# A trunk of two decoder layers on one core: the first group's queries and keys projected in one pass over the input tiles

## The chip, the cores and the metric

The kernel runs on one core of a Trainium2 chip. The metric is the device time of one execution in microseconds (us); the time of a kernel is the median of its runs. TensorE (PE) multiplies, VectorE (DVE), ScalarE (ACT) and GpSimd (POOL) do the rest, and all loads of the part that matters here are issued by SyncE (SP).

## What is computed

Two layers, 512 positions, width 1024, in float32. The first layer has stick-breaking heads and differential heads side by side, the second dilated attention; each layer ends in a squared-ReLU MLP and a gated embedding. Cut to what the change touches:

```
hn   = rmsnorm(h, norm_mix_g[i])
proj = hn @ w_in                      # 1024 -> 3072, split in qa, ka, va, qb, kb, vb
sc   = einsum('bqhmd,bkhmd->bhmqk', qb_b, kb) * scale
bias = table[t5_bucket(rel)]          # T5 bucket table, 32 x 16
prob = softmax(where(rel >= 0, sc + bias, NEG))
attn = prob[:, :, 0] - lam * prob[:, :, 1]
o_d  = rmsnorm(einsum('bhqk,bkhd->bqhd', attn, vb), subln_g) * (1 - lambda_init)
```

## The kernel before

Everything lies transposed: `h` is eight tiles of 128 channels x 512 positions. For float32 accuracy each operand is split in a high and a low part of type fp32r (`hi`/`lo` for inputs, `wh`/`wl` for weights; L187/L188, L122/L126/L128), and `mm3` (L141, L144, L145) forms three products: high x high, low x high, high x low. The high part is a copy on ACT, the low part a subtraction on DVE, or on POOL for weights of the mixer after the first blocks. The norm's factor is not applied to `h`; the products run on unnormed tiles, and the inverse root `rstd` is multiplied in when an accumulator is evacuated.

A layer's mixer works in four groups (`GROUPS`), each with 256 columns of queries, keys and values; `project` yields a group's products, `attend` the steps of its attention, and `interleave` writes the steps of one group among the products of the next. The first group (a differential one) has nothing to stand beside. Its order:

- The lead, at the level of `trunk`: SP loads `gcols`, then the eight input tiles and between them the queries' block in three chunks (1 MB); ACT and DVE split what has landed (L187, L188, L330, L331).
- `queries_keys`: two query accumulators over all eight tiles (`outer`, tile by tile), then `prepare`, then the key block (a load of its own, 1 MB, L114, split by L122 and L128) in two accumulators one after the other. Behind the first of them stands `statistics`: the squares (L250, L263) and two products with a matrix of ones (L272, L273), then the inverse root (L215 to L221).
- `prepare` makes the bias table: a product of the T5 table with one-hot rows (L351), written to DRAM (`urow`, L354), from where `load_bias` (L543) reads it with a shift.
- `evacuate` takes the four accumulators in turn: L495 multiplies by `rstd` into `tmp`, of which there is one buffer; for queries two copies and two subtractions follow (L501, L502), for keys four copies and two subtractions (L511 to L513).
- `values` (L447 on): the value block in two halves, the inverse root turned into columns before the second (`tok_cols`), four copies into `v` (L463, L464; tag "v", two buffers).
- The first `attend` steps stand among the value products of the second group: scores (L534, L535; two PSUM banks), softmax (L551, L554, L601 to L604).

Weight tiles have three buffers (tags "wh", "wl"), staging tiles two ("raw"). The lines of it that matter most:

```
start and isq: yield from lin_units(accs, blk, ahl, 0, KT, True)   # queries, tile by tile
prepare()
for i, acc in enumerate(accs):                                     # keys, one after the other
    yield from lin_units([acc], [blk[i]], ahl, 0, KT, False)
    if waiting:
        statistics()
        for x, held in enumerate(waiting):
            evacuate(True, x, held, qk, qscale)
```

The scheduler sets the order on each engine; it is printed below where the change moves it.

Of the kernel before, what the change touches and what calls it, by code (L numbers as in the profile page):

```python
# [12 lines left out]
F32 = mybir.dt.float32  # L13
# [6 lines left out]
P = 128  # L20
# [42 lines left out]
def trunk(  # L63
# [114 lines left out]
    def split_tile(src, scale=None, bufs=8, behind=()):  # L178
# [7 lines left out]
        else:  # L186
            last_split[:] = [nc.scalar.activation(hi, src, AF.Copy, scale=scale).ins]  # L187
            nc.vector.scalar_tensor_tensor(lo, src, scale, hi.bitcast(F32), op0=ALU.mult, op1=ALU.subtract)  # L188
# [126 lines left out]
    raw0 = wpool.tile([P, 2 * KT * P], F32, tag="raw", name=nm("raw"), bufs=2)  # L315
    raw0v = raw0.rearrange("p (i k c) -> p i k c", i=2, k=KT)
    src0 = w_in[0, 0].rearrange("p (i k c) -> p i k c", i=2, k=KT)
    blk0 = [tuple(wpool.tile([P, KT, P], F32R, tag=t, name=nm(t), bufs=3) for t in ("wh", "wl")) for _ in range(2)]
    chunks = {0: slice(0, 2), 1: slice(2, 4), 3: slice(4, 8)}
    nc.sync.dma_start(gcols, gvec)  # L320
    for k in range(KT):
        nc.sync.dma_start(h[k], xT[k])
        if k in chunks:
            nc.sync.dma_start(raw0v[:, :, chunks[k]], src0[:, :, chunks[k]])
    for k in range(KT):
        norm.done(k, stats=False)
        if k in chunks:
            for i, (hi, lo) in enumerate(blk0):
                ck = chunks[k]
                nc.scalar.activation(hi[:, ck], raw0v[:, i, ck], AF.Copy)  # L330
                nc.vector.tensor_tensor(lo[:, ck], raw0v[:, i, ck], hi[:, ck].bitcast(F32), op=ALU.subtract)  # L331
# [4 lines left out]
    def prepare():  # L336
        a, b, c, d = (mix[0].tile([P, S], F32, tag="bias", name=nm("prep"), bufs=4) for _ in range(4))
        lamt = t2k("tmp")[:, 0:4 * HD].rearrange("p (j c) -> p j c", j=4)
# [9 lines left out]
        for c0, src, offm in ((0, a[0:32], (b[0:16], c[0:16])),  # L348
                              (512, d[0:32, 0:128], (d[0:16, 128:256], d[0:16, 256:384]))):
            up = ps("pv" if c0 == 0 else "tp")[0:16, 0:src.shape[-1]]  # L350
            nc.tensor.matmul(up, d[0:32, 384:400], src, start=True, stop=True)  # L351
# [41 lines left out]
    def mixer(layer, norm, nxt):  # L393
# [12 lines left out]
        for t in pth + ptl:  # L406
            nc.gpsimd.memset(t[:, 11, :].bitcast(F32), 0.0)
        pt_i = [0]

        ahl = norm.parts()  # L410
        stat = {}

# [751 lines left out]
```

## Time and profile before

| | us |
|---|---|
| median of 3 runs (1294.65 to 1295.68) | 1295.13 |
| the profiled execution | 1294.86 |
| its span, first to last instruction | 1293.1 |
| PE busy | 1275.4 (99%) |
| DVE busy | 1003.9 (78%) |
| ACT busy | 709.5 (55%) |
| POOL busy | 212.9 (16%) |

The span is what the profile shows of the execution; some 1.8 us lie around it. Busy times are sums over instructions, and a busy engine need not be the one that sets the end: that is told by the chain that ended last and by what an engine waited for.

### The profile page before, as it was taken

The numbers are of one execution on the slowest core, as the hardware profiler recorded it, in microseconds if no ns is written. First come the engines' busy times: TensorE is split into PE (matmuls) and PEld (weight loads), VectorE is DVE, ScalarE is ACT, GpSimd is POOL, SyncE is SP. The second block draws the span as 40 slices with busy tenths as digits, with TensorE's granted clock in tenths as the row PEclk, the third lists the DMA queues.
The fourth block names the chain that finished last, engine by engine and source line by source line (L and its number), as shares of the span: only waits on it lengthen the run. The fifth ranks groups of instructions, "written<-read, shape, count | busy, mean of one in ns | idle before, by whom it ended". The sixth has DMA issues, their size and how long they took to land.

```text
span 1293.1 us, 19313 instructions
## 1 busy us (share of the span) xinstructions
PE 1275.4 (99%) x7520; PEld 1124.2 (87%) x7520; DVE 1003.9 (78%) x1666; ACT 709.5 (55%) x1146; POOL 212.9 (16%) x184
## 2 busy tenths in 40 slices
PE   9999999999999999999999999999999999999996
PEld 7988887888988989989889888788899898898986
DVE  6788798778848869779767777887785795986976
ACT  6667868555535335356456666765554443534544
POOL 2433434400000000001024333222000000000201
PEclk9999999999999999999999999999999999999999
DMA  6321423222222222638432222212323223255751
GB/s 211 144 82 54 159 75 114 90 98 98 95 102 98 98 98 98 195 107 219 140 127 86 82 90 75 73 58 80 116 98 101 95 99 115 82 148 146 173 178 66
DMA packets 33995, 144.25 MB, mean 112 GB/s; under 512 B 3888, under 2 KB 4624, under 8 KB 21232
## 3 DMA queue, kind: packets, MB, share of 16 engines
q1 hardware_dynamic: 29680, 135.16, 30.9%
q0 software_dynamic: 4224, 7.87, 3.6%
q8 instruction: 59, 0.97, 0.3%
q14 instruction: 32, 0.26, 0.1%
HBM read 131.92 MB, written 6.37 MB: 107 GB/s over the span
## 4 chain that ended last, share of the span: by engine, by line
PE 87%; DVE 7%; ACT 3%; issue 1%; DMA 0%; SPq 0%; POOL 0%; DVEq 0%; ACTq 0%; POOLq 0%
PE mm L141 11%; PE mm L144 11%; PE mm L145 11%; PE sc L144 6%; PE sc L145 6%; PE sc L141 5%; PE pv L145 5%; PE pv L144 5%; PE pv L141 5%; PE tp L145 4%; PE tp L144 4%; PE tp L141 4%; PE pv L581 3%; PE tp L560 2%; PE tp L900 2%
## 5 line engine op out<-in xcount | busy, mean ns | idle before, releaser
L122 ACT ACTIVATE wh<-raw 128x1024 fp32r<-128x1024 f32 (+1 forms) x156 | 160.5, 1034 | 142.6 <-PE mm L144 54.5
L126 POOL TENSOR_TENSOR wl<-raw,wh 128x512 fp32r<-128x512 f32 (+1 forms) x132 | 178.2, 1372 | 303.4 <-ACT wh L122 303.4
L141 PE MATMUL mm<-hi,wh 128*128 128x512 f32 x472 | 187.1, 396 | 0.6 <-DVE tmp L495 0.4
L145 PE MATMUL mm<-hi,wl 128*128 128x512 f32 x472 | 184.8, 391 | 0.1
L144 PE MATMUL mm<-lo,wh 128*128 128x512 f32 x472 | 184.6, 391 | 0.0
L128 DVE TENSOR_TENSOR wl<-raw,wh 128x1024 fp32r<-128x1024 f32 x90 | 109.5, 1223 | 39.6 <-ACT wh L122 34.1
L145 PEld LDWEIGHTS mm<-hi,wl 128*128 128x128 f32 x472 | 88.6, 188 | 20.0 <-POOL wl L126 0.5
L141 PEld LDWEIGHTS mm<-hi,wh 128*128 128x128 f32 x472 | 88.7, 188 | 17.5 <-DVE tmp L495 0.8
L144 PEld LDWEIGHTS mm<-lo,wh 128*128 128x128 f32 x472 | 88.8, 188 | 15.5
L784 POOL DMA_DIRECT2D s<-in_w_down_dram x4 | 4.5, 1123 | 578.7 <-DMA s<-in_w_down_dram 312.9
L813 ACT ACTIVATE wh<-s 128x1024 fp32r<-128x1024 f32 x58 | 61.1, 1054 | 54.5 <-DVE s L800 14.7
L554 ACT ACTIVATE e<-e,mn 128x128 f32<-128x128 f32 (+3 forms) x96 | 53.8, 561 | 62.5 <-DVE mn L551 62.2
L775 DVE TENSOR_TENSOR ul<-u,uh 128x1792 fp32r<-128x1792 f32 x32 | 64.8, 2024 | 29.4 <-ACT uh L774 29.2
L814 DVE TENSOR_TENSOR wl<-s,wh 128x1024 fp32r<-128x1024 f32 x58 | 70.9, 1222 | 16.6 <-ACT wh L813 16.3
L774 ACT ACTIVATE uh<-u 128x1792 fp32r<-128x1792 f32 x32 | 54.5, 1702 | 45.9 <-DVE u L772 45.9
L763 ACT ACTIVATE u<-u 128x512 f32<-128x512 f32 x64 | 39.7, 626 | 68.1 <-DVE u L762 68.1
L144 PE MATMUL sc<-lo,wh 128*128 128x512 f32 x184 | 72.0, 392 | 0.8 <-DVE lo L188 0.6
L141 PE MATMUL sc<-hi,wh 128*128 128x512 f32 x184 | 71.9, 391 | 0.7 <-ACT hi L187 0.7
L145 PE MATMUL sc<-hi,wl 128*128 128x512 f32 x184 | 71.8, 390 | 0.0
L141 PE MATMUL mm<-wh,hi 128*128 128x256 f32 (+1 forms) x216 | 63.3, 293 | 0.0
L145 PE MATMUL mm<-wh,lo 128*128 128x256 f32 (+1 forms) x216 | 63.0, 292 | 0.0
L144 PE MATMUL mm<-wl,hi 128*128 128x256 f32 (+1 forms) x216 | 62.9, 291 | 0.0
(308 smaller groups left out, 3884.5 us busy)
## 6 DMA issues: line engine op xcount, KB each, us to landing
raw<-in_w_up_dram SPq DMA_DIRECT2D x32, 1024.0 KB, 4.9
raw<-in_w_down_dram SPq DMA_DIRECT2D x32, 1024.0 KB, 4.9
raw<-in_w_in_dram SPq DMA_DIRECT2D x23, 1024.0 KB, 4.9
raw<-in_w_gate_dram SPq DMA_DIRECT2D x8, 1024.0 KB, 4.9
bias<-urow SPq DMA_DIRECT2D x24, 256.0 KB, 3.6
raw<-in_w_outa_dram SPq DMA_DIRECT2D x8, 768.0 KB, 4.2
pj<-pjd SPq DMA_DIRECT2D x16, 256.0 KB, 4.8
h<-in_xT_dram SPq DMA_DIRECT2D x8, 256.0 KB, 5.8
```

The lines of the kernel that those rows point to most:

```text
L122: act = nc.scalar.activation(hi, src, AF.Copy)
L126: nc.gpsimd.tensor_tensor(lo[:, kx], src[:, kx], hi[:, kx].bitcast(F32), op=ALU.subtract)
L128: last_low[:] = [nc.vector.tensor_tensor(lo, src, hi.bitcast(F32), op=ALU.subtract).ins]
L141: mm = nc.tensor.matmul(acc, lh, rh, start=start, stop=False)
L144: nc.tensor.matmul(acc, lh, rl, start=False, stop=False)
L145: return mm.ins, nc.tensor.matmul(acc, ll, rh, start=False, stop=stop).ins
L554: nc.scalar.activation(e[:, 0:n], e[:, 0:n], AF.Exp, scale=-1.0, bias=mn, accum_out=s)
L763: chain.append(nc.scalar.activation(ui, ui, AF.Square, scale=0.5).ins)
L774: nc.scalar.activation(uh, u, AF.Copy)
L775: part = nc.vector.tensor_tensor(ul, u, uh.bitcast(F32), op=ALU.subtract)
L813: high[:] = [nc.scalar.activation(hi, src, AF.Copy).ins]
L814: low[:] = [nc.vector.tensor_tensor(lo, src, hi.bitcast(F32), op=ALU.subtract).ins]
```

## The change

The first group's four weight blocks (two of queries, two of keys) are loaded in chunks between the input tiles, queries and keys in turn, and PE takes all four accumulators tile by tile. Two of the four split blocks lie in the buffers of the tag "v", in which the value tile follows later. `prepare` is cut in two: the loads and conversions stay ahead, and the product of the table, now in fp32r with the table split in high and low part, comes behind the 96 products of queries and keys, followed by `statistics`. The four evacuations come after that.

```
+    LOADS = (("h", 0, 1), ("w", 0, 2), ("h", 1, 2), ("w", 2, 4), ("h", 2, 4), ("w", 4, 8), ("h", 4, 8))
+    def lead_loads(mpool):
+        nc.sync.dma_start(gcols, gvec)
+        raws = [wpool.tile([P, 2 * KT * P], F32, tag="raw", name=nm("raw"), bufs=2) for _ in range(2)]
+        views, parts = [], []
+        for raw in raws:
+            views.append(raw.rearrange("p (k i c) -> p i k c", i=2, k=KT))
+            parts.append([wpool.tile([P, KT, P], F32R, tag=t, name=nm(t), bufs=3) for t in ("wh", "wl")])
+            both = mpool.tile([P, QT, 512], F32R, tag="v", name=nm("wv"), bufs=2).rearrange(
+                "p (x a) b -> p x (a b)", x=2).rearrange("p x (k c) -> p x k c", k=KT)
+            parts.append([both[:, x] for x in range(2)])
...
+        for what, a, b in LOADS:
+            if what == "h":
+                for k in range(a, b):
+                    nc.sync.dma_start(h[k], xT[k])
+            else:
+                cols = slice(a * 2 * P, b * 2 * P)
+                for x, raw in enumerate(raws):
+                    nc.sync.dma_start(raw[:, cols], w_in[0, x][:, cols])
+        for what, a, b in LOADS:
+            if what == "h":
+                for k in range(a, b):
+                    norm.done(k, stats=False)
+                    in_turn(*last_split)
+            else:
+                for x, (hi, lo) in enumerate(parts):
+                    src = views[x // 2][:, x % 2, a:b]
+                    act = nc.scalar.activation(hi[:, a:b], src, AF.Copy)
+                    in_turn(act.ins, nc.vector.tensor_tensor(lo[:, a:b], src, hi[:, a:b].bitcast(F32), op=ALU.subtract).ins)
+        return parts, list(ahead)
...
 def prepare():
-            nc.tensor.matmul(up, d[0:32, 384:400], src, start=True, stop=True)
...
+        nc.vector.tensor_copy(onr[0:32], a[0:32])
+        nc.vector.tensor_copy(endr[0:32, 0:128], d[0:32, 0:128])
+        nc.vector.tensor_copy(th, d[0:32, 384:400])
+        nc.vector.tensor_tensor(tl, d[0:32, 384:400], th.bitcast(F32), op=ALU.subtract)
...
+        def rest():
...
+                nc.tensor.matmul(up, th, src, start=True, stop=False)
+                nc.tensor.matmul(up, tl, src, start=False, stop=True)
...
 def queries_keys():
+                if start and not layer:
+                    rest = prepare()
+                    accs = [ps(lead_in.pop(0)) for _ in range(4)]
+                    yield from lin_units(accs, lead, ahl, 0, KT, True)
+                    rest()
+                    statistics()
+                    for i, acc in enumerate(accs):
+                        evacuate(i < 2, i % 2, acc, qk, qscale)
+                    return
...
             if start:
                 yield from queries_keys()
-                yield from values()
-            else:
-                yield from values()
+            v = value_tile()
+            cur.extend((g, kind, v, heads))
+            yield from values()
+            if not start:
                 yield from queries_keys()
```

The change moves instructions on the engines. Three places follow, of before first and of the change behind it; line numbers of the change are some 40 higher from `prepare` on.

First place: PE at the end of the first group's queries (before), and at the end of its queries and keys (after). `sc` are the query accumulators, `mm` the key accumulators, `pv` and `tp` banks for the table, the norm and the values, `hi`/`lo` numbers stand for input tiles.

```order
L141 MATMUL sc_208<-hi_173,wh_119 128x512
L144 MATMUL sc_208<-lo_174,wh_119 128x512
L145 MATMUL sc_208<-hi_173,wl_120 128x512
L351 MATMUL pv_281<-prep_269,prep_272 16x512
L351 MATMUL tp_287<-prep_272 16x128
L141 MATMUL mm_267<-hi_133,wh_259 128x512
L144 MATMUL mm_267<-lo_134,wh_259 128x512
L145 MATMUL mm_267<-hi_133,wl_260 128x512
```

```order
L141 MATMUL mm_252<-hi_212,wv_145 128x512
L144 MATMUL mm_252<-lo_213,wv_145 128x512
L145 MATMUL mm_252<-hi_212,wv_145 128x512
L389 MATMUL pv_349<-tmp_48_228,tmp_49_229 16x512
L390 MATMUL pv_349<-tmp_48_228,tmp_49_229 16x512
L389 MATMUL tp_356<-tmp_49_229 16x128
L390 MATMUL tp_356<-tmp_49_229 16x128
L273 MATMUL tp_386<-e_387,ones_r 128x512
L274 MATMUL tp_386<-e_388,ones_r 128x512
L141 MATMUL pv_438<-wh_440,hi_160 128x256
```

The keys' products stood behind the table's; now they stand among the queries', and the table's four products and the norm's two (L273, L274) follow all of them, right ahead of the values.

Second place: DVE from the evacuation of the first key tile (L495, now L539, `tmp<-mm`) to the first softmax step (L551, now L595). `klz` is a key's low part, `v` the value tile, `rcol` the norm's factor as columns.

```order
L495 SCALAR_TENSOR_TENSOR tmp_376<-mm_267,rstd_324 128x512
L513 TENSOR_TENSOR klz_182<-tmp_376,kh_378 64x512
L513 TENSOR_TENSOR klz_184<-tmp_376,kh_382 64x512
L297 TENSOR_SCALAR rcol_487<-tp_482 128x4
L495 SCALAR_TENSOR_TENSOR tmp_410<-mm_268,rstd_324 128x512
L513 TENSOR_TENSOR klz_183<-tmp_410,kh_412 64x512
L513 TENSOR_TENSOR klz_185<-tmp_410,kh_416 64x512
L464 SCALAR_TENSOR_TENSOR v_206<-pv_422,rcol_487,v_206 128x256 x2
L464 SCALAR_TENSOR_TENSOR v_206<-tp_423,rcol_487,v_206 128x256 x2
L551 ISA e_591,mn_592<-sc_588,bias_582 128x128
```

```order
L539 SCALAR_TENSOR_TENSOR tmp_415<-mm_251,rstd_363 128x512
L501 SCALAR_TENSOR_TENSOR v_435<-pv_438,rcol_503,v_435 128x256
L557 TENSOR_TENSOR klz_121<-tmp_415,kh_417 64x512
L557 TENSOR_TENSOR klz_123<-tmp_415,kh_421 64x512
L539 SCALAR_TENSOR_TENSOR tmp_425<-mm_252,rstd_363 128x512
L501 SCALAR_TENSOR_TENSOR v_435<-pv_438,rcol_503,v_435 128x256
L501 SCALAR_TENSOR_TENSOR v_435<-tp_439,rcol_503,v_435 128x256
L557 TENSOR_TENSOR klz_122<-tmp_425,kh_427 64x512
L557 TENSOR_TENSOR klz_124<-tmp_425,kh_431 64x512
L595 ISA e_607,mn_608<-sc_604,bias_598 128x128
L595 ISA mn_608 128x1
L595 ISA e_614,mn_615<-sc_611,bias_600 128x128
```

The four value copies stood behind both key tiles; now the first stands behind the reading of the first key tile, two behind the reading of the second, and the fourth, two rows below the last one shown, behind the first softmax step.

Third place: ACT at the copies of the second key tile (L511, L512, now L555, L556) and of the values.

```order
L512 ACTIVATE kh_382<-tmp_376 64x512
L122 ACTIVATE wh_645<-raw_546 128x1024
L511 ACTIVATE kh_412<-tmp_410 64x512
L512 ACTIVATE kh_412<-tmp_410 64x512
L511 ACTIVATE kh_416<-tmp_410 64x512
L512 ACTIVATE kh_416<-tmp_410 64x512
L463 ACTIVATE v_206<-pv_422,rcol_487 128x256 x2
L463 ACTIVATE v_206<-tp_423,rcol_487 128x256
L122 ACTIVATE wh_778<-raw_776 128x1024
```

```order
L555 ACTIVATE kh_421<-tmp_415 64x512
L556 ACTIVATE kh_421<-tmp_415 64x512
L500 ACTIVATE v_435<-pv_438,rcol_503 128x256
L500 ACTIVATE v_435<-tp_439,rcol_503 128x256
L122 ACTIVATE wh_794<-raw_792 128x1024
L555 ACTIVATE kh_427<-tmp_425 64x512
L556 ACTIVATE kh_427<-tmp_425 64x512
L555 ACTIVATE kh_431<-tmp_425 64x512
L556 ACTIVATE kh_431<-tmp_425 64x512
L500 ACTIVATE v_435<-tp_439,rcol_503 128x256
```

The split of the second group's queries (`wh_778`, now `wh_794`) stood behind three value copies; now it stands ahead of the second key tile's copies. The split that stood there before (`wh_645`) has moved up among the queries' copies.

## Rows read from the trace of the kernel before

**Rows 1.** Page, part 4: the chain that ended last, shares by engine.
```profile
PE 87%; DVE 7%; ACT 3%; issue 1%; DMA 0%; SPq 0%; POOL 0%; DVEq 0%; ACTq 0%; POOLq 0%
```
**Rows 2.** Waits of PE over the span: us in total, times, longest us.
```profile
PE sc L534 <- DVE mn L551: 0.7, 2, 0.5
```
**Rows 3.** Windows: us, PE busy, PEld, DVE, ACT, POOL, PEclk, DMA share, GB/s.
```profile
59.30:1293.10 1233.80, 1219.57 (x7181) 1075.50 (x7181) 961.51 (x1580) 671.84 (x1078) 192.46 (x156) 1.00 0.34 108
```
**Rows 4.** Chain in order of time, 25 to 60 us: start us, us, what.
```profile
25.94 1.06 ACT wh L122
...
31.06 0.70 DVE tmp L495
...
33.17 0.70 DVE qq L502
...
36.11 1.68 DVE qq L502
...
37.89 0.70 DVE tmp L495
...
39.92 0.63 ACT kh L511
...
44.23 1.68 DVE klz L513
...
45.95 0.50 DVE v L464
...
49.05 0.28 DVE e L551
...
59.28 0.36 PE sc L534
```
**Rows 5.** Timeline of PE, 0 to 50 us: start us, us, operation [idle before].
```profile
5.42 0.50 PE L141 MATMUL sc<-hi,wh 128*128 128x512 f32 x1
...
19.15 1.03 PE L351 MATMUL pv<-prep,prep 32*16 32x512 f32 x2
...
20.33 0.50 PE L141 MATMUL mm<-hi,wh 128*128 128x512 f32 x1
...
25.91 0.40 PE L272 MATMUL tp<-e,ones_r 128*128 128x512 f32 x1
26.16 0.40 PE L273 MATMUL tp<-e,ones_r 128*128 128x512 f32 x1
26.39 0.40 PE L141 MATMUL mm<-hi,wh 128*128 128x512 f32 x1
...
31.88 0.28 PE L141 MATMUL pv<-wh,hi 128*128 128x256 f32 x1
...
49.39 0.39 PE L534 MATMUL sc<-kh,qq 128*128 128x256 f32 x1
```
**Rows 6.** Timeline of ACT, 0 to 27 us.
```profile
7.00 0.72 ACT L187 ACTIVATE hi<-h,gcols 128x512 fp32r<-128x512 f32 x1 [1.33 <-DMA h<-in_xT_dram]
8.14 0.72 ACT L330 ACTIVATE wh<-raw 128x256 fp32r<-128x256 f32 x2 [0.42 <-DMA raw<-in_w_in_dram]
...
11.04 1.15 ACT L330 ACTIVATE wh<-raw 128x512 fp32r<-128x512 f32 x2 [0.87 <-DMA raw<-in_w_in_dram]
...
26.91 0.67 ACT L215 ACTIVATE rstd<-tp,eps_n 128x512 f32<-128x512 f32 x1
```
**Rows 7.** Timeline of POOL, near 34 us.
```profile
34.23 3.00 POOL L126 TENSOR_TENSOR wl<-raw,wh 128x512 fp32r<-128x512 f32 x2 [3.76 <-ACT wh L122]
```
**Rows 8.** DMA issues from 0 to 45 us: count, KB each, us to landing.
```profile
bias<-urow SPq DMA_DIRECT2D x4, 256.0 KB, 6.1
...
urow<-prep SPq DMA_DIRECT2D x2, 32.0 KB, 4.4
```
**Rows 9.** Timeline of DVE, 7 to 42 us.
```profile
7.76 0.75 DVE L188 SCALAR_TENSOR_TENSOR lo<-h,gcols,hi 128x512 fp32r<-128x512 f32 x1 [1.54 <-ACT hi L187]
...
41.50 0.69 DVE L495 SCALAR_TENSOR_TENSOR tmp<-mm,rstd 128x512 f32<-128x512 f32 x1
```

More of the change, by code (lines that the diff above doesn't have):

```diff
@@ L314, in trunk @@
     norm = Norm(0, 0)
[L315 to L331, printed above, removed]
+    LOADS = (("h", 0, 1), ("w", 0, 2), ("h", 1, 2), ("w", 2, 4), ("h", 2, 4), ("w", 4, 8), ("h", 4, 8))
[9 more added lines that the diff above has]
+            parts.append([both[:, x] for x in range(2)])
+        ahead = []
+        def in_turn(*pair):
+            for later, earlier in zip(pair, ahead):
+                order(later, earlier)
+            ahead[:] = pair
+        for what, a, b in LOADS:
[17 more added lines that the diff above has]
+        return parts, list(ahead)
@@ L361, in prepare @@
         nc.vector.tensor_scalar(gsub, gcols[:, 48:49], -0.5 * (D // P) * (1.0 - LAMBDA_INIT), None, op0=ALU.mult)
+        def rest():
+            for c0, src, offm in ((0, onr[0:32], (b[0:16], c[0:16])),
+                                  (512, endr[0:32, 0:128], (d[0:16, 128:256], d[0:16, 256:384]))):
+                up = ps("pv" if c0 == 0 else "tp")[0:16, 0:src.shape[-1]]
+                nc.tensor.matmul(up, th, src, start=True, stop=False)
+                nc.tensor.matmul(up, tl, src, start=False, stop=True)
+                for l in range(2):
+                    nc.vector.scalar_tensor_tensor(offm[l], up, -1.0, offm[l], op0=ALU.mult, op1=ALU.add)
+                    nc.sync.dma_start(urow[l, :, c0:c0 + src.shape[-1]], offm[l])
+        return rest
     pjd = dpool.tile([DEPTH, KT, P, S], F32, tag="pjd", name="pjd")
@@ L408, in mixer @@
         pt_i = [0]
+        if not layer:
+            lead, lead_end = lead_loads(mpool)
         ahl = norm.parts()
@@ L415, in statistics @@
                 for k in range(KT):
-                    norm.stats(k, last_split)
+                    norm.stats(k, lead_end[:1])
             stat["rstd"] = norm.finish(use_tables(sig_tail) if layer else None)
-        nblk = [0]
+        nblk = [0 if layer else 2]
         def next_block():
@@ L432, in project, with value_tile @@
             first.append(g)
-            v = mpool.tile([P, QT, 512], F32R, tag="v", name=nm("v"), bufs=2)
+            def value_tile():
+                return mpool.tile([P, QT, 512], F32R, tag="v", name=nm("v"), bufs=2)
             def values():
@@ L473, in queries_keys @@
                     lo_eng[0] = nc.vector if start else nc.gpsimd
-                    blk = blk0 if isq and start and not layer else block(src, KT, P)
+                    blk = block(src, KT, P)
                     lo_eng[0] = nc.gpsimd
@@ L480, in queries_keys @@
                         continue
-                    if start and not layer:
-                        prepare()
                     for i, acc in enumerate(accs):
```

16 lines of the change are left out of this document (6 added, 10 removed).

## Prediction

> **What bounds the kernel now.** I read four views in this order. The shares of the chain that ended last give PE 87% [rows 1], so most of the span is TensorE working without a break, and only a place where the chain leaves PE can give time back. The waits of PE over the whole span are few and short; the one that matters here is at the first scores, on DVE, 0.7 us in all [rows 2]. The windows say the same: from 59.3 us on PE is busy 1219.57 of 1233.80 us [rows 3].
>
> The chain in order of time is the view that decides. It leaves PE at 25.9 us and comes back to it only at 59.28 [rows 4]. In between it runs over ACT and DVE: the norm's inverse root, then the four evacuations of queries and keys (L495 at 31.06 and 37.89 for the first query and the first key tile; the second key tile begins at 41.50 [rows 9]), then four copies of values from 45.95, then the first softmax step at 49.05. They follow one another because the evacuations share one "tmp" buffer. PE is busy meanwhile, with keys and values, but it has no slack at the end of it: the second score step starts at 49.39 [rows 5], as soon as the first softmax step has read its bank, and at 59.28 PE really waits, 0.5 us. So an earlier PE is worth nothing here by itself; the time of the kernel moves with the ACT/DVE chain, and that chain starts at the matmul of the norm's sum of squares.
>
> **The change, part by part.**
>
> *Loads.* 4 MB instead of 3 MB go out in the lead; SP issues one transfer after the other as before. I read when the n-th transfer is usable from the ACT rows that waited for a DMA: the third quarter MB at 7.00 us, the fourth at 8.14, 2 MB at 11.04 [rows 6]. Now the third is the first chunk of the keys and the fourth is input tile 1. h0 and the queries' first chunk keep their place, so the first product stays at 5.42 [rows 5].
>
> *PE in the lead.* Before, 48 products (two accumulators) run from 5.42 to the table products at 19.15, and 48 more from 20.33 to 31.88, with 0.48 for the norm's two between. At the pitch of the undisturbed part, (25.91 - 20.33) / 24 or (31.88 - 26.39) / 24, about 0.229 us, 48 take 11.0; so the lead stalls 19.1 - 5.4 - 11.0 = 2.7 us. After, tile 0 has 12 products. Six run to 6.9. The keys' chunk lands at 7.0, its high part takes 0.4, the products go on at 7.4 and, held by the low parts, end near 8.8. Tile 1 lands at 8.14, its high part takes 0.72 [rows 6] and its low part 0.75 [rows 9]: 9.6. PE then has eleven more products: 12.1. Each of the other six tiles takes 12 x 0.229 = 2.75; the split of 2 MB by 11.04 plus two splits is ready by 12.1, and the later ones run ahead of PE by my addition. End: 12.1 + 6 x 2.75 = 28.6.
>
> *The bias table.* Before, two fp32 products went as four and cost 20.33 - 19.15 = 1.18 us. Now they are four fp32r products. No row has one of 32 rows; the bounds are 1.18 (each as before) and 2 x 0.229 + 2 x 0.06 = 0.58 by columns at the pitch above. I take 0.6, since the nearest row is the fp32r product of 512 columns. The four new conversions on DVE lie beside PE's products and cost nothing; uncovered they would be about 1 us, and they stand in front of the sums of squares, which are done by my addition near 25.4, 3 us before PE asks.
>
> *Start of the values and of the chain.* 28.6 + 0.6 + 0.48 = 29.7 us for the first value product, against 31.88: PE is 2.2 ahead. But the norm's products, which stood between the two key accumulators (second one at 26.16 [rows 5]), now come after all 96. Its first ACT step began at 26.91 [rows 6], held by a weight split; it can now begin at 29.85. **The chain starts 2.94 us later.**
>
> *The chain itself.* From the root's first step to the first evacuation it took 31.06 - 26.91 = 4.15 and for two queries 37.89 - 31.06 = 6.83. One thing in it changes: POOL's runs of weight lower parts. A subtraction of 64x512 takes 0.70 free (33.17) and up to 1.68 when a POOL run is in the way (36.11 [rows 4], POOL at 34.23 [rows 7]). POOL's runs shift with the value blocks; by my addition two more of the root's steps are held and one or two query subtractions fewer. I take +0.5 for the root and -0.3 for the queries; the bounds are -0.6 and +1.0 together (one held step is worth 1.68 - 0.70 = 0.98).
>
> *Value copies.* In the old order on DVE all four stood behind the last key tile: 49.05 - 45.95 = 3.1 us. In the new order (the second place shown with the change) three of them stand between the evacuations, where DVE waits for ACT anyway, and the fourth behind the first softmax step. Against that a weight split of ACT, 1.06 (as at 25.94 [rows 4]), now stands between the reading of the second key tile and its four copies (the third place); the split that stood there before ran while DVE was not yet at that tile. First to second key tile was 41.50 - 37.89 = 3.61, I take -0.2. Second key tile to softmax was 49.05 - 41.50 = 7.55; it becomes 0.70 + 1.06 + three copies of 0.63 (39.92) + a last subtraction of 0.70 to 1.68 = 4.3 to 5.3. I take the held one, as at 44.23 [rows 4]: -2.2; the other end is -3.2.
>
> The Trainium skill ("SBUF — State Buffer", Who interferes with whom) says that a DVE instruction with two SBUF inputs and a GpSimd instruction that reads SBUF exclude each other for a whole instruction, whoever started first. The row at 36.11 agrees. By the rule the last subtraction is the 1.68 one and the sum stays; by a free row it would be 1.0 lower.
>
> *Rows moved past queues.* On SP three weight blocks instead of two now stand ahead of the writes of the bias table. The third waits until POOL has done the values' second half, near 32.5, so the writes go at 33 to 35; with 4.4 to land and 6.1 for the four loads behind them [rows 8] the first pair is there by 46, and needed near 49.8. Cost nothing; were that cover gone, each us late is a us of time.
>
> *Sum at the first softmax step:* +2.94 + 0.5 - 0.3 - 0.2 - 2.2 = **+0.7 us**, i.e. 49.8 instead of 49.05. PE arrives about 2.2 early, waits some 3 us there and goes on 0.7 late. All behind it is in the old order and PE-bound. The profiled execution took 1294.86 us, 0.27 under the median of the three runs: 1294.86 + 0.7 = 1295.5. With the ends (chain -1.1 to +0.5 around what I took, last subtraction -1.0 to 0, landings and table 0.7 earlier to 1.2 later) it is 1292.8 to 1297.3.
>
> **Rivals.**
>
> 1. *PE's lead gets through.* If the chain stops being the bound, PE keeps its 2.2 and the 0.5 it waited at 59.28: 1294.86 - 2.7 = 1292.2. For it: the value copies do leave the chain. Against it: the first softmax step would have to come by about 46.9, 2.9 earlier than I add up, more than all low ends together. Chance 0.13.
> 2. *POOL decides, slower.* POOL's runs now follow one another almost without a gap from 27 to 35 us, under the root and the first query. Ten DVE steps of the chain read SBUF twice, two in the root and eight subtractions. If three more than I counted are held, 3 x 0.98 = 2.9 comes on top: 1298.4. It decides from three on; against it, steps that read PSUM (the evacuations) are never slow in the profile. Chance 0.06.
> 3. *The change does nothing to the order.* Excluded for the order (the first place shows the keys' products among the queries'); only late landings could undo it: if input tiles 4 to 7 come after 17.6 us, when PE asks for the first of them, each us late is a us on the chain. After 2 MB at 11.04 that leaves 6.5 us for 1.25 MB, which took 4.04 between 7.00 and 11.04. With tiles two us late it would be 1297.5. Chance 0.04.
>
> **How the numbers follow.** A measurement of this kernel can tell about 0.2%, 2.6 us, from no change: 1292.5 to 1297.7 is "same". The forecast has the remaining 0.77, all of it within these bounds, as is rival 3. Rival 1 lies beyond the lower bound, rival 2 beyond the upper one; 0.01 more goes to each side for landings that I misread. So faster 0.14, same 0.79, slower 0.07. The forecast's own range is 1292.8 to 1297.3; with its upper end at 1297.5, where rival 3 lies, what is left out is rivals 1 and 2, 0.19.
>
> **What would show it.** In the profile after: 96 products without a long gap from about 9 us, first value product near 29.7, the norm's first ACT step near 29.9, first softmax step at 49.8 (49 to 51), and a new wait of about 3 us of PE at the first or second scores or at the second value bank of the next group, on DVE. If PE has no such wait and the first softmax step stands before 47, the chain was shorter than I added up and rival 1 holds. If the first softmax step stands after 51.5 with subtractions above 1.3 us before it, rival 2 does.

## The result: 1.8 us slower in the median, the forecast chain 0.9 us longer in the profile

The kernel after took 1296.92 us (median of 17 runs, 1295.69 to 1299.15), the kernel before, run beside it, 1295.13 (17 runs): ratio 1.0015, 95% interval 1.0008 to 1.0022. That is inside the 0.2% called "same" and inside the range, and 1.4 us above the number. The profiled execution took 1296.31 us (span 1294.5), 1.45 over that of the kernel before.

The shares of the chain that ended last, of the kernel after, moved by one point from PE to DVE [rows 1]:

```profile
PE 86%; DVE 8%; ACT 3%; issue 2%; DMA 1%; POOL 0%; SPq 0%; DVEq 0%; ACTq 0%; POOLq 0%
```

PE's waits, kernel after (waiting product, engine and tile waited for: us in total, times, longest). The wait at the first scores has grown from 0.7 to 2.5 [rows 2]; the last row shown is the first product of the lead:

```profile
PE sc L578 <- DVE mn L595: 2.5, 3, 2.0
...
PE sc L141 <- ACT wh L352: 0.6, 1, 0.6
```

PE's timeline, kernel after (start, busy time, engine, line, operation; in brackets idle before and what ended it): first product, first product of the third input tile, first product of the bias table, first of the norm, first value product, second score step. They answer to [rows 5]:

```profile
6.62 0.50 PE L141 MATMUL sc<-hi,wh 128*128 128x512 f32 x1 [0.64 <-ACT wh L352]
...
12.28 0.39 PE L141 MATMUL sc<-hi,wh 128*128 128x512 f32 x1
...
29.07 0.40 PE L389 MATMUL pv<-tmp,tmp 32*16 32x512 f32 x1
...
29.76 0.50 PE L273 MATMUL tp<-e,ones_r 128*128 128x512 f32 x1
...
30.32 0.28 PE L141 MATMUL pv<-wh,hi 128*128 128x256 f32 x1
...
50.27 0.39 PE L578 MATMUL sc<-kh,qq 128*128 128x256 f32 x1 [1.99 <-DVE mn L595]
```

PE does begin the values 1.56 us earlier (30.32 against 31.88), and all of it is gone at the first scores, where it stands for 1.99 us. ACT's timeline, kernel after: the first weight chunk and the norm's two steps [rows 6]:

```profile
6.15 0.42 ACT L352 ACTIVATE wh<-raw 128x256 fp32r<-128x256 f32 x1 [1.33 <-DMA raw<-in_w_in_dram]
...
30.52 0.69 ACT L216 ACTIVATE rstd<-tp,eps_n 128x512 f32<-128x512 f32 x1 [1.23 <-PE tp L274]
31.24 0.63 ACT L219 ACTIVATE rstd<-rstd 128x512 f32<-128x512 f32 x1
```

DVE's timeline, kernel after: the first step of the root, first query, first key, second key, the last two subtractions, the first softmax step and the fourth value copy behind it. They answer to [rows 4] and [rows 9]:

```profile
31.91 0.76 DVE L220 TENSOR_TENSOR e<-rstd 128x512 f32<-128x512 f32 x1 [0.49 <-ACT rstd L219]
...
34.41 0.69 DVE L539 SCALAR_TENSOR_TENSOR tmp<-sc,rstd 128x512 f32<-128x512 f32 x1
...
41.16 0.69 DVE L539 SCALAR_TENSOR_TENSOR tmp<-mm,rstd 128x512 f32<-128x512 f32 x1
...
44.65 0.69 DVE L539 SCALAR_TENSOR_TENSOR tmp<-mm,rstd 128x512 f32<-128x512 f32 x1
...
46.84 3.05 DVE L557 TENSOR_TENSOR klz<-tmp,kh 64x512 fp32r<-64x512 f32 x2 [0.71 <-ACT kh L555]
49.92 0.29 DVE L595 CUSTOM_DVE_ANT_0 e<-sc,bias 128x128 f32<-128x128 f32 x1
...
50.35 0.48 DVE L501 SCALAR_TENSOR_TENSOR v<-tp,rcol,v 128x256 fp32r<-128x256 f32 x1
```

The sum, laid beside the forecast, from these starts:

| stretch of the chain | before | after | change | forecast |
|---|---|---|---|---|
| start of the norm's first ACT step | 26.91 | 30.52 | +3.61 | +2.94 |
| from there to the first query | 4.15 | 3.89 | -0.26 | +0.5 |
| first query to first key | 6.83 | 6.75 | -0.08 | -0.3 |
| first to second key | 3.61 | 3.49 | -0.12 | -0.2 |
| second key to softmax | 7.55 | 5.27 | -2.28 | -2.2 |
| first softmax step | 49.05 | 49.92 | +0.87 | +0.74 |

From there PE is behind by the same amount. Counted from the last product back, the same product starts at 94.08 us before and 94.88 after (+0.80); near 600 us the difference is 1.05, near 1200 1.54. The windows of the kernel after, from 60 us on (PE busy, then PEld, DVE, ACT, POOL, clock, DMA share, GB/s), against [rows 3]:

```profile
60.00:1294.50 1234.50, 1220.23 (x7181) 1076.02 (x7181) 961.80 (x1580) 672.34 (x1078) 192.54 (x156) 1.00 0.34 108
```

PE is idle there for 14.27 us, against 14.23 before. So no new wait stands behind the first scores. The 0.7 us between the product near 94 us and the end came in pieces far behind the change; they were not followed further, and their cause is open.

### The profile page after: what moved, and what is told of

Its sections match the earlier page's. It is cut to its first block, busy times and chain, and to the rows that moved or that the text cites. A ratio compares the mean times of both kernels' runs of the same rounds, so it can differ in the third digit from the quotient of the medians.

```text
span 1294.5 us, 19324 instructions
## 1 busy us (share of the span) xinstructions
PE 1275.7 (99%) x7520; PEld 1125.5 (87%) x7520; DVE 1004.1 (78%) x1674; ACT 710.9 (55%) x1150; POOL 212.8 (16%) x184
## 4 chain that ended last, share of the span: by engine, by line
PE 86%; DVE 8%; ACT 3%; issue 2%; DMA 1%; POOL 0%; SPq 0%; DVEq 0%; ACTq 0%; POOLq 0%
PE mm L141 11%; PE mm L144 11%; PE mm L145 11%; PE sc L141 5%; PE sc L144 5%; PE sc L145 5%; PE pv L145 5%; PE pv L141 5%; PE pv L144 5%; PE tp L145 4%; PE tp L144 4%; PE tp L141 4%; PE pv L625 3%; PE tp L604 2%; PE tp L944 2%
## 5 line engine op out<-in xcount | busy, mean ns | idle before, releaser
L141 PE MATMUL mm<-hi,wh 128*128 128x512 f32 x464 | 184.0, 396 | 0.6 <-DVE tmp L539 0.4
L145 PE MATMUL mm<-hi,wl 128*128 128x512 f32 x464 | 181.7, 392 | 0.1
L144 PE MATMUL mm<-lo,wh 128*128 128x512 f32 x464 | 181.4, 391 | 0.0
L819 DVE TENSOR_TENSOR ul<-u,uh 128x1792 fp32r<-128x1792 f32 x32 | 64.8, 2025 | 29.7 <-ACT uh L818 29.5
L141 PE MATMUL sc<-hi,wh 128*128 128x512 f32 x176 | 68.7, 390 | 0.6 <-ACT wh L352 0.6
L145 PE MATMUL sc<-hi,wl 128*128 128x512 f32 x176 | 68.7, 390 | 0.0
L144 PE MATMUL sc<-lo,wh 128*128 128x512 f32 x176 | 68.6, 390 | 0.0
```

Source lines behind the costliest of these rows:

```text
L141: mm = nc.tensor.matmul(acc, lh, rh, start=start, stop=False)
L144: nc.tensor.matmul(acc, lh, rl, start=False, stop=False)
L145: return mm.ins, nc.tensor.matmul(acc, ll, rh, start=False, stop=stop).ins
L819: part = nc.vector.tensor_tensor(ul, u, uh.bitcast(F32), op=ALU.subtract)
```

## The experiments

Theory: the first softmax step, the end of a chain over ACT and DVE, sets the time, and PE's lead is lost in front of it. Rival: PE, or something later, sets it, and where the softmax step stands is no matter. Each run was timed beside the kernel before on the same chip; "softmax" is the start of the first softmax step in the profiled execution (49.05 before, 49.92 after).

**e1_norm_late.** The kernel before with only the norm and the evacuations put behind both key accumulators, the one cost that the forecast gave to the change:

```diff
+                    if waiting and not layer:
+                        for i, acc in enumerate(accs):
+                            yield from lin_units([acc], [blk[i]], ahl, 0, KT, False)
+                        statistics()
+                        for i, acc in enumerate(waiting + accs):
+                            evacuate(i < 2, i % 2, acc, qk, qscale)
+                        continue
```

> The kernel before with one part of the change alone: the norm's two products and the four evacuations come behind both key accumulators, the loads and the order of the products stay. Theory (the ACT/DVE chain from the norm's products to the first softmax step sets the time): the chain starts at about 32.0 instead of 26.91, gets the three value copies into its gaps as in the changed kernel (-2.2), and the first softmax step comes at 51.5 to 52.5 instead of 49.05; the time is 2.5 to 3.4 us over the kernel before. Rival (PE's order of products in the lead, or the lead's loads, set the time): PE does the same products at the same times, so the first value product stays at 31.9 and the time is within 0.5 us of the kernel before.

Measured: 1297.65 us, ratio 1.0021 (1.0013 to 1.003). Softmax at 52.15, +3.10, within what was expected. DVE's timeline and PE's waits of this kernel:

```profile
49.08 3.05 DVE L520 TENSOR_TENSOR klz<-tmp,kh 64x512 fp32r<-64x512 f32 x2 [0.71 <-ACT kh L518]
52.15 0.29 DVE L558 CUSTOM_DVE_ANT_0 e<-sc,bias 128x128 f32<-128x128 f32 x1
```

```profile
PE sc L541 <- DVE mn L558: 2.5, 3, 2.0
```

The chain starts 5.94 us later (first ACT step of the norm at 32.85 for 26.91) and gets 2.29 us back behind the second key (46.89 to 52.15, 5.26 for 7.55). PE's order of products in the lead is that of the kernel before. So the forecast's cost and its largest saving are both shown, and the rival falls. Some 0.5 us of the 3.10 is not the norm's: this execution's first weight chunk landed late and its first products ran at half pace (both below), so that the first value product stands at 32.40 for 31.88.

**e2_tmp_two.** The kernel after with a second buffer for the evacuations, which breaks their being strung on one `tmp`:

```diff
-                f = t2k("tmp")
+                f = t2k("tmp2" if i and not layer and g == groups[0] else "tmp")
```

> The changed kernel with a second buffer for the evacuations of the first group (the second tile of each pair goes to the tag tmp2). Theory: the four evacuations no longer wait for one another, the first softmax step comes about 1.6 us earlier than in the changed kernel (48.3 instead of 49.92), and the time is 1.3 to 2 us under the changed kernel, some 0.5 to 1 under the kernel before. Rival (what the changed kernel lost was lost in the lead's loads and the later first product): the lead is the same, so the time stays at that of the changed kernel.

Measured: 1295.59 us, ratio 1.0002 (0.9993 to 1.001). Softmax at 49.07: 0.85 earlier than after, not 1.6. The root's first step shows the missing part:

```profile
32.16 1.70 DVE L220 TENSOR_TENSOR e<-rstd 128x512 f32<-128x512 f32 x1 [0.49 <-ACT rstd L219]
```

1.70 instead of 0.76, in a kernel whose edit comes behind that step: a step held by a POOL run, 0.94 us more. The first evacuation comes 0.93 later than in the kernel after (35.34 for 34.41), 0.25 of it because the norm does; behind it the chain is 1.78 shorter. How much of that is the broken string is open: POOL's runs lie elsewhere too (the one at 46.37 in the kernel after, beside the last pair of key subtractions, begins at 47.96 here, and the last key subtraction is free), and the value copies stand behind the last key subtraction again.

**e3_no_pool_low.** The kernel after without the subtractions for the first six weight splits whose lower part falls to POOL; those lower parts are left out of the products (the high part is read in their place):

```diff
-        if lo_eng[0] is nc.gpsimd:
+        if lo_eng[0] is nc.gpsimd and n_low[0] < 6:
+            n_low[0] += 1
+            lo = hi
+        elif lo_eng[0] is nc.gpsimd:
```

> The changed kernel without the first six weight subtractions on POOL: the low parts of the first values' block, of the second group's values and of its queries are left out, and the high part is read in their place, so PE's products keep their number and size. Theory: DVE's steps between the norm and the first softmax step are all free of POOL, some 3 us less in sum (the last pair of subtractions 1.4 instead of 3.05, the second query pair 1.4 instead of 2.49, the root 0.3 less), and the first softmax step comes at 46.8 to 47.3; PE then is the bound and keeps its 1.6 us of lead, and the time is 2 to 3 us under the changed kernel and 1 to 2 under the kernel before. Rival (POOL is not in the way, the single buffer alone makes the length): the first softmax step stays within 0.7 us of 49.92.

Measured: 1294.3 us, ratio 0.9991 (0.9982 to 1.0), softmax at 47.33. DVE's timeline of this kernel, the rows that answer to those at 31.91 and 46.84 of the kernel after:

```profile
31.79 0.69 DVE L223 TENSOR_TENSOR e<-rstd 128x512 f32<-128x512 f32 x1 [0.49 <-ACT rstd L222]
...
45.30 0.68 DVE L560 TENSOR_TENSOR klz<-tmp,kh 64x512 fp32r<-64x512 f32 x1 [0.71 <-ACT kh L558]
46.61 0.69 DVE L560 TENSOR_TENSOR klz<-tmp,kh 64x512 fp32r<-64x512 f32 x1 [0.62 <-ACT kh L558]
47.33 0.29 DVE L598 CUSTOM_DVE_ANT_0 e<-sc,bias 128x128 f32<-128x128 f32 x1
```

No DVE step of the chain is held any more, and the chain is 2.6 us shorter. So POOL's work, which is off the chain, costs it 2.6 us. By the rule of the Trainium skill that the prediction names (SBUF — State Buffer, Who interferes with whom) the held steps are those with two SBUF inputs beside a POOL run. This run agrees: without those runs they take 0.68 to 0.69 us.

**e4_norm_early.** The kernel after with the norm's products behind the seventh input tile:

```diff
-                    yield from lin_units(accs, lead, ahl, 0, KT, True)
+                    for x, cost in enumerate(lin_units(accs, lead, ahl, 0, KT, True)):
+                        if x == 27:
+                            statistics()
+                        yield cost
                     rest()
-                    statistics()
```

> The changed kernel with the norm's two products put among the products of queries and keys, behind the seventh input tile, as soon as the sums of squares are ready; the table's products stay behind all of them. Theory: the chain starts at about 26.8 instead of 30.52, loses 1 us to a weight split ahead of its second step and 1 to the table's additions on DVE, so the first evacuation comes at 32.8 instead of 34.41 and the first softmax step at 48.3; the time is about 1.6 us under the changed kernel and 0.5 to 1 under the kernel before. Rival (the lead's loads or PE's order cost the time): PE's lead is the same and the time stays at that of the changed kernel.

Measured: 1297.11 us, ratio 1.0013 (1.0004 to 1.0022), no gain, so the theory missed; the time is the rival's, but for other reasons than PE's order. The norm's first ACT step comes 3.9 us earlier (26.61), the softmax step only 0.34 (49.58). ACT's timeline of this kernel tells where the first part went:

```profile
26.61 0.69 ACT L216 ACTIVATE rstd<-tp,eps_n 128x512 f32<-128x512 f32 x1 [0.71 <-PE tp L274]
27.20 1.05 ACT L122 ACTIVATE wh<-raw 128x1024 fp32r<-128x1024 f32 x1
28.15 0.62 ACT L219 ACTIVATE rstd<-rstd 128x512 f32<-128x512 f32 x1
```

The root's second step now stands behind a weight split, its next one is held by POOL (28.80, 1.54), the table's additions stand between two others, and POOL holds a pair of query subtractions for 3.08. And the execution is longer than its softmax step says: at 94 us PE is 1.99 behind the kernel before, with 0.53 on the chain, 1.46 more. Windows of this kernel (window, length, then busy us and count of PE, PEld, DVE, ACT, POOL, the granted clock, DMA share, GB/s):

```profile
48.00:50.00 2.00, 0.06 (x1) 0.06 (x1) 1.97 (x4) 0.98 (x3) 1.00 (x1) 1.00 0.00 0
50.00:52.00 2.00, 2.00 (x11) 2.00 (x12) 1.59 (x7) 0.80 (x4) 0.00 (x0) 0.59 0.00 0
52.00:54.00 2.00, 2.00 (x12) 2.00 (x12) 1.11 (x7) 1.86 (x5) 0.00 (x0) 0.55 0.00 0
```

PE stood for 2 us, and when it went on it was granted about half its clock, the 1.2 GHz level, for (0.41 + 0.45) x 2 x 2 = 3.4 us, which costs half of that, 1.7.

**e5_pe_filled.** The kernel after with work for PE in that wait:

```diff
+                if n == 1 and not layer and g == groups[0]:
+                    fill = ps("pv")
+                    for _ in range(4):
+                        nc.tensor.matmul(fill[:, 0:P], ident, ident, start=True, stop=True)
```

> The kernel after, with four fp32 128x128 products of the identity (8 rows of PE, about 1.6 us by the rows of transposes) put on PE right ahead of the second score step of the first group, where PE otherwise stands for 2.0 us; their result is never read. Theory (the runs of the kernel after above 1297.5 us are those in which the granted clock fell behind that stand): the work lies in the stand and costs nothing on the chain, so the profiled time stays at 1296.3 +-0.5 and first softmax at 49.9; the runs above 1297.5, 8 of 17 before, become rare, and the median comes down by 0.5 to 1 us to 1296.0 to 1296.4. Rival (PE decides the time there, the stand is no slack): every run is 1.6 us later, median 1298.5. Second rival (the two modes have another cause): median and share of high runs stay as with the kernel after, 1296.9.

Measured: 1296.41 us, ratio 1.001 (1.0001 to 1.0019). The work took 1.05 us at 48.70 (1.6 was expected), and the wait behind it fell from 1.99 to 1.08. So the wait was slack: the rival of 1298.5 falls. One run of 11 is above 1297.5 (after: 8 of 17), as expected; e9 below, with the whole wait, has two of 11, so this alone is weak. The profiled execution, 1297.43, is outside its forecast: softmax at 50.48, 0.56 late, of which 0.32 stood already at the norm's product (30.08) and 0.24 is a longer hold of L220 (1.00 for 0.76).

**e6_lows_dve, e8_norm_early_two, e7_lows_dve_norm_early.** Three versions that shorten the chain by what the runs above had found. All have the second buffer of e2. e6 adds the first two lines below (the value block's low parts on DVE while PE is in the lead), e8 the norm and the table early, e7 both:

```diff
+                    lo_eng[0] = nc.vector if start and not layer else nc.gpsimd
...
+                    lo_eng[0] = nc.gpsimd
...
-                    yield from lin_units(accs, lead, ahl, 0, KT, True)
-                    rest()
-                    statistics()
+                    for x, cost in enumerate(lin_units(accs, lead, ahl, 0, KT, True)):
+                        if x == 23:
+                            rest()
+                        if x == 27:
+                            statistics()
+                        yield cost
```

> The kernel after, with a buffer of its own for the second tile of each pair of evacuations and the low parts of the first group's value weights subtracted on DVE instead of POOL; everything is computed. Theory (POOL's subtractions are what holds DVE's subtractions; DVE has room under PE's 96 products): no DVE step of the chain above 1.1 us, the eight low parts cost DVE 8 x 0.7 = 5.6 us that lie beside products; first softmax at 47.6 (46.8 to 48.3), 2.3 before that of the kernel after; PE waits under 0.7 us at the scores; profile 1294.0 to 1294.8, median 0.9985 to 0.9995 of the kernel before. Rival (DVE becomes the bound: the low parts stand between the steps of the chain): first softmax at 50 to 52, time at or above that of the kernel after, 1297.

> The kernel after with the buffer of its own for each second tile, the table's products behind the sixth input tile and the norm's behind the seventh; POOL's subtractions unchanged. Theory (three terms of the chain add up: norm 1.6 earlier less what ACT's splits and POOL hold, buffer 0.85 earlier): first softmax at 48.0 to 48.6, profile 1294.3 to 1294.9, median of the kernel before within 0.05%. Rival (POOL's runs set the chain wherever the norm stands): first softmax at 49.0 to 49.6 as with the second buffer alone or with the early norm alone, 1295.5 or more.

> The same as e6_lows_dve, with the table's products behind the sixth input tile and the norm's two products behind the seventh instead of behind all 96. Theory (the chain from the norm's products bounds, until it is earlier than PE): the first softmax step comes earlier than in e6_lows_dve by 0.5 to 2 us, at or before the end of PE's value products at 47.8; PE's lead then gets through, PE waits under 0.3 us at the scores, 1.6 to 2.1 us under the kernel before, median 1293.2 to 1293.8, ratio 0.9984 to 0.9988. Rival (the chain holds on ACT: the inverse root stands behind weight splits as in e4_norm_early): first softmax as in e6_lows_dve +-0.3 and the same time as there.

Measured: e6 1293.99 us, ratio 0.9991 (0.9982 to 1.0), softmax 47.96; e8 1293.78, ratio 0.999 (0.9981 to 0.9999), softmax 48.48; e7 1292.97, ratio 0.998 (0.9971 to 0.9989), softmax 47.17. All three softmax steps stand where expected; the medians of e7 and e8 are a little better than that. Two forecasts missed: e8's profiled execution, 1295.05, is above its 1294.9, and in e6 PE waits 0.8 us in all at the scores and a pair of key subtractions is still held (2.25 for two). DVE's timeline of e7, first step of the root, the four query subtractions and the softmax step, all free:

```profile
31.03 0.69 DVE L220 TENSOR_TENSOR e<-rstd 128x512 f32<-128x512 f32 x1
...
35.37 2.83 DVE L551 TENSOR_TENSOR qq<-tmp,qq 64x512 fp32r<-64x512 f32 x4
...
47.17 0.28 DVE L600 CUSTOM_DVE_ANT_0 e<-sc,bias 128x128 f32<-128x128 f32 x1
```

One key subtraction of e7 is still held (1.54, at 39.62). PE's first value product of e7, 1.09 ahead of the kernel before (31.88):

```profile
30.79 0.28 PE L141 MATMUL pv<-wh,hi 128*128 128x256 f32 x1
```

The windows of e7, against the 9.40 of 10 us that PE was busy there in the kernel after:

```profile
50.00:60.00 10.00, 10.00 (x73) 9.39 (x71) 7.80 (x29) 7.71 (x23) 2.56 (x2) 1.00 0.42 148
```

PE does not wait at the first group's scores any more (the one wait at scores left is 0.2 us, at 94.70), and its lead gets through: **e7 is 4 us under the kernel after and 2.2 under the kernel before, with an interval that lies below 1.**

**e12_best_again, e11_best_halved, e9_first_chunk_halved, e10_keys_chunk_later.** The first product had come 1.2 us later than forecast. e9 (on the kernel after) and e11 (on e7) halve the first chunks; e10 (on the kernel after) puts the keys' first chunk behind input tile 1, where "0" and "1" are the queries' and the keys' block alone; e12 is e7 unchanged, on the chip of e11:

```diff
-    LOADS = (("h", 0, 1), ("w", 0, 2), ("h", 1, 2), ...
+    LOADS = (("h", 0, 1), ("w", 0, 1), ("w", 1, 2), ("h", 1, 2), ...    # e9, e11
+    LOADS = (("h", 0, 1), ("0", 0, 2), ("h", 1, 2), ("1", 0, 2), ...    # e10
```

> The kernel after, with the first chunk of queries and of keys (256 KB each) loaded and split as two of 128 KB each, so that what is in flight before the first product is as many bytes as in the kernel before. Theory (the first product stands 1.2 us later than forecast because two chunks are in flight together, and in the kernel after everything up to the first softmax step hangs on it, since PE works without a stall from there to the norm's products): first product at 5.4 to 5.9, first value product 0.7 to 1.2 earlier than 30.3, norm's first ACT step and first softmax step 0.4 to 1.2 earlier (48.7 to 49.5), profile 1295.2 to 1295.9. Rival (the splits on ACT and DVE set the pace of the first tiles): first product earlier, but PE then stalls for the second chunk or tile 1, first value product at 30.3 +-0.3 and the time that of the kernel after.

> The kernel after, with the first chunk of the keys loaded and split behind input tile 1 instead of right behind the queries' first chunk (undoes the alternate order of that one chunk). Theory (one chunk in flight lands as in the kernel before): first product at 5.4 +-0.2, six products to 6.8, then a stall of 1.5 to 2.2 until the keys' chunk is split near 8.6, then no stall: 8.6 + 90 x 0.232 = 29.5 for the end of the 96 against 28.9, first value product 30.9 (30.5 to 31.5), first softmax 0.2 to 1.2 later than 49.92, profile 1296.5 to 1297.5. Rival (landing does not hang on what else is in flight): first product at 6.6 as in the kernel after, and the end of the 96 above 30.

> The kernel of e7_lows_dve_norm_early (buffer of its own for second tiles, value lows on DVE, table's products behind the sixth tile and the norm's behind the seventh) with the first chunks loaded in halves as in e9_first_chunk_halved. Theory (there PE works without a stall from its first product to 60 us and sets the time, so an earlier first product gets through whole): 0.7 to 1.2 us below e7_lows_dve_norm_early, median 1291.8 to 1292.4, ratio to the kernel before 0.9972 to 0.998; PE's wait at the first scores under 0.5 us. Rival (ACT and DVE, which now do the value lows as well, bound the first tiles): the time of e12_best_again +-0.3.

> The kernel of e7_lows_dve_norm_early unchanged, for a comparison with e11_best_halved on one chip and a second measurement of its gain: ratio to the kernel before 0.9975 to 0.9988 if the gain of the first measurement (0.998, interval 0.9971 to 0.9989) is its own; 0.999 or above if it was luck.

Measured: e9 1296.96 us, ratio 1.0013 (1.0004 to 1.0022), softmax 51.38; e10 1297.78, ratio 1.0019 (1.001 to 1.0028), softmax 51.96; e11 1292.64, ratio 0.998 (0.9971 to 0.9989), softmax 47.16; e12 1293.25, ratio 0.9983 (0.9974 to 0.9991), softmax 47.95. e12 confirms the gain of e7. The softmax steps of e9 and e10 came later than expected (48.7 to 49.5, and 50.1 to 51.1), and e11 gained 0.61 us on e12 for 0.7 to 1.2.

The theory of the landings falls, in two ways. Smaller chunks bring the first product forward (5.75 in e9 and e11), but tile 1 then lands at 8.13 and 8.48, PE waits for it, and the values begin at 30.82 and 30.77, no earlier than with whole chunks (30.20 to 30.65 in the other kernels with e9's order of products, 30.79 in e7); e11 and e12 differ by less than their runs spread (1.38 and 2.23). And in e10, with one chunk in flight as before, the first product stands at 6.12, not 5.4. What settles that a landing is no fixed time is e1, which has the loads of the kernel before, unchanged. ACT's timeline of e1, beside 4.95 in [rows 6] for the same chunk:

```profile
6.35 0.72 ACT L330 ACTIVATE wh<-raw 128x256 fp32r<-128x256 f32 x2 [1.80 <-DMA raw<-in_w_in_dram]
```

The same loads land 1.4 us apart in two executions; why is open. So it is with the keys' first chunk in e7 (usable at 7.31) and e12, whose ACT and PE timelines show it:

```profile
8.45 0.42 ACT L352 ACTIVATE wh<-raw 128x256 fp32r<-128x256 f32 x1 [1.80 <-DMA raw<-in_w_in_dram]
```

```profile
8.92 0.50 PE L141 MATMUL mm<-hi,wh 128*128 128x512 f32 x1 [0.52 <-ACT wh L352]
```

That execution begins its values 0.78 later than e7's (31.57 against 30.79), and is 0.75 later at 94 us.

e10 shows something else: undoing the alternate order of one chunk makes PE wait 1.53 us for the keys, puts the norm 1.37 later (31.13) and the softmax step 2.04; the other 0.68 is the root's stretch (4.57 for 3.89), in which L220 is held for 1.71. Against the five executions with the loads and the norm's place of the kernel after (norm at 29.64 to 30.08) the norm is 1.0 to 1.5 later: that is what the alternate chunks are worth to this change.

**All profiled executions together.** The shift of the first softmax step against the kernel before, and that of the same product near 94 us:

| | softmax | at 94 us | | softmax | at 94 us |
|---|---|---|---|---|---|
| after | +0.87 | +0.80 | e7 | -1.88 | -1.98 |
| e1 | +3.10 | +3.01 | e8 | -0.57 | -0.56 |
| e2 | +0.02 | -0.08 | e9 | +2.33 | +2.24 |
| e3 | -1.72 | -1.93 | e10 | +2.91 | +2.81 |
| e4 | +0.53 | +1.99 | e11 | -1.89 | -2.01 |
| e5 | +1.43 | +1.32 | e12 | -1.10 | -1.23 |
| e6 | -1.09 | -1.17 | | | |

In ten of these kernels PE waits for DVE at the first group's scores (the longest wait is 0.3 to 2.0 us). In nine of them the two shifts agree within 0.21 us, over 4.6 us of range; the exception, e4, is the execution with the fallen clock. That is the theory shown for them: the first softmax step sets when PE goes on. In e7, e11 and e12 PE has no such wait, and the agreement is not the softmax step's doing: there the product near 94 us moves with PE's own first value product (-1.09, -1.11 and -0.31), and is 0.9 us further ahead in each, 0.5 of it the wait at 59.28 that is gone.

From that product to the end the executions drift. The shift of the whole profiled execution differs from that near 94 us by -0.5 (e10) to +1.25 us (e5), +0.65 in the kernel after. So the table shows what sets the time up to 94 us, and a single execution's time is no measure of it to better than about a microsecond.

## Why the prediction was right, and where its steps were not

- *What bounds:* right. The table above is its evidence, with the wait of 1.99 us on DVE, and e1 that of its first cost.
- *"The first product stays at 5.42":* this step failed, and it hardly cost the sum. It read one execution's landing as a fixed time; the chunk was usable at 6.15 after, and between 5.65 and 6.35 in the ten other executions that load it whole. But the forecast also had stalls in the first two tiles, until 12.1. In their place PE ran without a stall from 6.62, and the third tile began at 12.28. That a late first product moves the norm is not shown: e9's came at 5.75 and its norm later (30.25 for 29.76).
- *The pitch of the lead:* this was mis-sized, and is the largest part. The 72 products of the other six tiles took 16.79 (12.28 to 29.07) for 16.5, 0.233 each; of its two readings, 0.2325 and 0.229, the prediction had taken the lower one.
- *The bias table:* 0.69 (29.07 to 29.76) for 0.6; the conversions lay beside products, as said. With the norm's 0.56 for 0.48 the first value product came at 30.32 for 29.7, and the norm's first ACT step at 30.52 for 29.85. So the term +2.94 measured +3.61: 0.18 at the first two tiles, 0.29 of pitch, 0.09 and 0.08 for table and norm, 0.03 behind them.
- *The root, +0.5 for steps held by POOL:* -0.26 in the profiled execution, where L220 took 0.76. It is no fixed size: in e2, e5, e9 and e10, which have the norm in the same place, L220 took 1.70, 1.00, 1.74 and 1.71, and the stretch 4.57, 4.13, 4.86 and 4.57, which is +0.42, -0.02, +0.71 and +0.42. With the queries' term the executions without a second buffer stand at -0.34 (after), -0.10, +0.63 and +0.33 (e5, e9, e10), all between the forecast's ends for the two together, -0.6 and +1.0.
- *Queries, second key, value copies:* -0.08, -0.12 and -2.28 for -0.3, -0.2 and -2.2. The copies and the moved weight split stand as forecast; the last pair of subtractions was held as a whole (3.05, 0.7 each when free). In e3, where they are free, the stretch takes 4.21, near the forecast's other end, 4.3.
- *Sum:* +0.87 for +0.74, mainly by errors of +0.67 and -0.76 that cancel; that the sum came so near was luck, the size of the root's hold above all. PE's wait at the first scores was 1.99 us for some 3: of the 2.2 that it should have been ahead it had 1.56 at the first value product and 1.22 at the first score step (45.85 for 47.07).
- *SP's queue and the writes of the bias table:* no wait of DVE or PE in the chain was put down to them, as forecast.
- *The number:* 1295.5 held for the chain, not for the profiled execution (1296.31; 0.65 of the 0.81 above it arose behind 94 us) and not for the median. The forecast took one execution for all; the runs of the kernel after spread over 3.5 us, those of the kernel before over 1.6 beside them (2.6 at most on any chip). Three things seen in the profiles lengthen single executions: late landings (0.78 at the first value product, e12 against e7), a held L220 (0.7 to 1.0 of the root's stretch, e2, e9 and e10), and the clock (1.7 in e4). How the 17 runs divide among them is open, since one of them was profiled.
- *Rivals:* the first did not hold, for the reason that was given: the softmax step would have had to come by 46.9. e7 brings it to 47.17 by other edits; PE's lead then gets through, and the time, 1292.97, is near the rival's 1292.2. The second, that POOL holds three more steps than counted, stands in no profile: the root and the queries took at most 0.63 more than before (e9), where the rival needs some 3. Whether it did in the runs that were not profiled is open. The third did not occur.
- *Not tried:* two split blocks in the value tiles' ring, since without them the four blocks don't fit; no wait in the profiles was put down to that ring.

## What to carry to other kernels

Before work is moved to give the matrix engine a lead, find the chain that it has to meet at the next place where it waits, and move that chain's start first: here PE's lead of 1.6 us at the values ended in a loss of 1.8 us in the kernel after, and a lead of 1.1 us in a gain of 2.2 in e7, where the norm stands one tile earlier, a second buffer breaks the string of evacuations, and most of POOL's subtractions are out of the way. An engine off the chain can lengthen it without ever being waited for: look for rows of one shape that take 0.70 in one place and 1.68 in another. And where a term is the time at which a first transfer lands, take its spread from several executions, not its value from one, and ask whether a stall behind it absorbs it.

## What was not expected of the hardware

The clock. Where PE stands for some 2 us at the first scores, one profiled execution went on at the 1.2 GHz level (e4's windows above); the same stand in the profiled executions of after, e1, e9 and e10 was followed by a clock of 1.00 throughout. The runs agree with this as the cause of longer ones, without proving it. Split by mean granted clock, 0.998 against 0.997 or less, the means of the runs are 2.15 us apart in e1 (7 and 4 runs), 1.50 in e4 (2 and 9), 1.24 in the kernel after (10 and 7), 1.11 in e9 (5 and 6) and 0.52 in e10 (7 and 4), all with a wait of 2.0. They are 0.06 apart in the kernel before (61 and 38 runs) and not above 0.1 in e5 and e2, where the longest wait there is 1.1 and 1.2; in e7, without a wait, they are 0.6 apart, which landings can make as well, and 0.3 or less in e3, e6, e8, e11 and e12. A fall of 3.4 us to half would take 0.0013 off the mean.

The start is uneven as well: in some executions the first products run at half pace (seven of them in e1, three in e11). The windows show a granted clock of 1.00 there, so what slows them is open. PE's timeline of e11, first products of the lead, 0.43 apart instead of 0.23:

```profile
6.33 0.63 PE L144 MATMUL sc<-lo,wh 128*128 128x512 f32 x1
6.75 0.63 PE L145 MATMUL sc<-hi,wl 128*128 128x512 f32 x1
7.18 0.61 PE L141 MATMUL sc<-hi,wv 128*128 128x512 f32 x1
```
